# Prompt attention in five stages instead of four, with the queries normalized ahead of the logits' operations

## The chip, the core and the metric

The kernel runs on one core of a Trainium2 chip. The core has a matrix engine (TensorE, PE in the profile, with its weight loads as PEld), VectorE (DVE), ScalarE (ACT), GpSimd (POOL) and SyncE (SP), whose queue issues the DMAs. Each engine works through its own list of instructions and waits on semaphores for the others. The metric is the device time of one execution in microseconds (us), lower is better.

## The reference

One layer of a hybrid decoder, for a prompt of 2048 positions and for eight single samples. What matters here is the prompt's sliding-window attention with 16 heads of 64 in 4 groups. In short:

```python
h = rmsnorm(x, norm_g) * (1 + scale) + shift
q, k, v, ga, xr, gr, ma, mr = split(h @ w_in)           # 1024, 256, 256, 1024, 1024, 1024, 1024, 1024 columns
q = rmsnorm(q.reshape(B, T, 16, 64), q_g)                # per head
k = rmsnorm(k.reshape(B, T, 4, 64), k_g)
logits = q . k * 64**-0.5                                # keys of the own and of the previous 128-block
logits = where(0 <= dist < 128, logits + rel_bias(dist), -1e30)
p = softmax(concat(logits, sink))[..., :-1]              # one sink logit per head
o = p @ v
ya = o * silu(ga)
hs = rglru(causal_conv(xr)); yr = hs * silu(gr)
y = x + gate * ((sigmoid(ma) * (ya @ w_pa) + sigmoid(mr) * (yr @ w_pr)) @ w_out)
```

The layer also returns the last 128 keys and values, the convolution's last rows and the recurrence's last state, and the same for the samples, whose attention runs over a window of 128 cached keys.

## The kernel before

The prompt is worked through in two halves of 1024 positions, the samples along with the second. A half begins with the keys and values (`phase_kv`), goes on with the attention (`phase_attn`), and then with a long line of matmul pieces for the gates, the recurrence and the output (`stages`, `line`). Matmul operands are kept in two parts, a rounded high part and the rest, and each product is three matmuls (high by high, high by low, low by high).

The attention works on 32 tiles: 4 pairs of two heads in each of two groups (`u`) by 8 blocks of 128 positions (`tt`). Its loop is a software pipeline written out by hand: one **turn** `i` of the loop does one stage each for several tiles, and inside the attention every instruction is kept in the order in which the loop writes it, on each engine. A tile's stages are:

- `gemm_a`, `stage_a1`: 24 matmuls make the queries of tile i in a `pg` bank; ScalarE squares them, VectorE sums the squares (the **reduction**), and GpSimd makes the **factor** of the norm in two operations (`rstd_of`, the second one a power).
- `stage_a2`: VectorE's **normalization**, the queries times their factor, out of the `pg` bank into an `H` tile.
- `stage_b1`: TensorE transposes the normalized queries, ScalarE makes the high part, VectorE the low part (the **split queries**).
- `stage_b2`: 12 matmuls make the **logits** in two `pq` banks. The pool `pq` has two banks, so a tile takes both.
- `stage_b0`, `stage_b3`: GpSimd copies the sinks into a tile; then the **logits' operations** on VectorE, two masked copies and four additions of the bias with a running extreme (with an accumulator read each), and four exponentials on ScalarE.
- `stage_b4`: VectorE's **reciprocal** of the sums and GpSimd's **product** of the probabilities with it.
- `stage_c1`, `stage_c2`: transposes of the probabilities, their masked copies, and the values' matmuls.

Turn i of the loop writes, in this order: `stage_b4` of tile i - 2, splitting of weights that are due (`weights`), `stage_b0` of tile i - 1, q matmuls and `stage_a1` of tile i, `stage_b1` of tile i - 1, `stage_c1` of tile i - 3, `stage_c2` of tile i - 4, filler matmuls (`fill`), `stage_b2` and `stage_b3` of tile i - 1, `stage_a2` of tile i. The filler is the attention's gate, cut into 12 halves of 12 matmuls of 512 columns; the list `want` says how many are done by the end of each turn. The weights of the next 256 query columns are split in turns 4 to 7, 12 to 15 and 20 to 23 (one ScalarE and one VectorE operation in each), those of the last gate column group at the start of turn 31. In the last turns the loop also emits pieces of the line that follows (`line.emit`). In the second half, `stage_s` puts the samples' queries in: at the end of the turns with tt = 2, 4, 6 and 7 it issues a step of them behind the logits' operations.

Of the kernel before, what the change touches and what calls it, by code (L numbers as in the profile page):

```python
# [41 lines left out]
def tile_hybrid_step(ctx: ExitStack, tc: tile.TileContext, x_prompt, x_sample, cache_k, cache_v, state_conv,  # L42
# [27 lines left out]
    cp = ctx.enter_context(tc.tile_pool(name="cp", bufs=1))  # L70
    sp = ctx.enter_context(tc.tile_pool(name="sp", bufs=1))
    bp = ctx.enter_context(tc.tile_pool(name="bp", bufs=1))
    hp = ctx.enter_context(tc.tile_pool(name="hp", bufs=6))
    mp = ctx.enter_context(tc.tile_pool(name="mp", bufs=16))
    dp = ctx.enter_context(tc.tile_pool(name="dp", bufs=1, space=DRAM))
    pg = ctx.enter_context(tc.tile_pool(name="pg", bufs=3, space=PSUM))
# [480 lines left out]
    def phase_attn(s, hT, sa, kT, vt, chunks, line):  # L557
# [9 lines left out]
        def stage_a2(ps, ss):  # L567
            qn = H([2, 2, HD])
            V.tensor_tensor(qn, ps[:, :256].rearrange("p (gg j d) -> p j gg d", gg=2, j=2),
                            ss.rearrange("p (gg j) -> p j gg", gg=2).unsqueeze(3).broadcast_to([P, 2, 2, HD]),  # L570
                            op=ALU.mult)
            return qn

        def stage_b1(u, tt, qn):
            Gp = u // 2
            if tt == 0 and s > 0:
                kcs[u] = [H([256], F32R), H([256], F32R)]
                for kc, car, cur in zip(kcs[u], (KCh, KCl), kT[Gp]):
                    A.copy(kc[:, 0:P], car[:, Gp, :])
                    A.copy(kc[:, P:256], cur[:, 0:P])  # L580
            p2 = PT()
            for jl in range(2):
                T_.transpose(p2[:, jl * P:(jl + 1) * P], qn[:, jl].rearrange("p g d -> p (g d)"), ident)
            qh, ql = H([2, P], F32R), H([2, P], F32R)
            src = p2[:, :256].rearrange("p (j c) -> p j c", j=2)
            A.activation(qh, src, AF.Identity, scale=qg)
            V.scalar_tensor_tensor(ql, src, qg, qh.bitcast(F32), op0=ALU.mult, op1=ALU.subtract)
            return qh, ql
# [44 lines left out]
        def stage_b4(lt, sm):  # L633
            V.reciprocal(sm, sm)
            G_.tensor_tensor(lt[:, :, 0:P], lt[:, :, 0:P], sm.unsqueeze(2).broadcast_to([P, 4, P]), op=ALU.mult)
            return lt

        def stage_c1(tt, lt):
            p3 = PT().rearrange("p (h q) -> p h q", h=4)
            for i in range(4):  # L640
                T_.transpose(p3[:, i, :], lt[:, i, 0:P], ident)
            free(lt)
            pc = Tt([4, P])
            if s == 0 and tt == 0:
                V.tensor_tensor(pc, p3, mcT4, op=ALU.mult)
                return [(vt[0][0][:, 0, :], pc)]
            pa = Tt([4, P])
            A.copy(pa, p3)
            V.tensor_tensor(pc, p3, mcT4, op=ALU.mult)
            return [(v_before(vt, tt), pa), (vt[1][tt // 2][:, tt % 2, :], pc)]  # L650
# [94 lines left out]

        gps = [None]
        nh = len(GA) * nt
        want = [4, 6, 6] + [2 * nt] * (N - 4) + [nh - 2] + [nh] * 4


        order = [(next(i for i in range(N) if want[i] > n * nt) if n > 1 else max(n - 1, 0), 0, 2, "g", f, 0, h)
# [13 lines left out]
        def weights(i, end):  # L765
            while order and order[0][:2] <= (i, end):
                kind, n, _, h = order.pop(0)[3:]
                dst = (wqs if kind == "q" else wga).setdefault(n, [])
                dst.extend(split_raw(raws[0], 256 if kind == "q" else 128, halves=(h,)))
                if h == 1:  # L770
                    if s == 1 and kind == "g":
                        raw = [r_.rearrange("p (k c) -> p k c", c=128) for r_ in raws[0]]
                        gsm.append(samples_gemm([raw[k // 4][:, k % 4, :] for k in range(KT)], P, hsF,
                                                (sgaS if n < KT else maS)[:, n % KT:n % KT + 1, :], PG,
                                                PT))
                        next(gsm[-1])
                    raws.pop(0)
                    prefetch()
# [10 lines left out]
        pend = yield  # L789
        pinned[0] = True  # L790
        weights(-1, 1)
        ps_, qn_, c_, sm_, lt_ = {}, {}, {}, {}, {}
        for i in range(N + 4):
            evacs = []
            gsm_ready = len(gsm)
            if 2 <= i <= N + 1:
                lt_[i - 2] = stage_b4(*sm_.pop(i - 2))
            weights(i, 0)
            if 1 <= i <= N:
                ub, tb = seq[i - 1]  # L800
                if tb == 0 and ub % 2 == 0:
                    mbs[ub // 2] = S([8, P])
                    ld.dma_start(mbs[ub // 2], Md[:, ub // 2 * 8:ub // 2 * 8 + 8])
                lt = stage_b0(ub)

            def fill(n):
                nonlocal hdone
                while hdone < n:
                    evacs.append(ga_half(hdone))
                    hdone += 1  # L810

            if i == N:
                fill(nh - 1)
            if i > N:
                line.emit(2 * (i - N - 1))
            if i < N:
                u, tt = seq[i]
                ps_[i] = PG()
                gemm_a(ps_[i], wqs[u], hT, tt * P)
                if s == 1 and tt == 2:  # L820
                    next(smp[u])
                if tt == 7:
                    drop(wqs.pop(u))
                ss = stage_a1(ps_[i])
            if 1 <= i <= N:
                b = stage_b1(ub, tb, qn_.pop(i - 1))
            if i:
                weights(i - 1, 1)
            if 3 <= i < N + 3:
                c_[i - 3] = stage_c1(seq[i - 3][1], lt_.pop(i - 3))  # L830
            if i < N and pend:
                next(pend.pop(0))
            if i > N:
                line.emit(2 * (i - N - 1) + 1)
            if i >= 4:
                u4, t4 = seq[i - 4]
                stage_c2(u4, t4, c_.pop(i - 4))
                if u4 == 3 and t4 % 2:
                    free(vt[1][t4 // 2])
                if t4 == 7:  # L840
                    for f in (2 * u4, 2 * u4 + 1):
                        st.dma_start(yad[s, f], ya[f])
                        free(ya.pop(f))
            fill(want[i])
            if 1 <= i <= N:
                sm_[i - 1] = stage_b3(ub, tb, stage_b2(ub, tb, *b), lt)
                if ub % 2 and tb == 7:
                    free(mbs.pop(ub // 2), *kT[ub // 2])
            if i < N:
                qn_[i] = stage_a2(ps_.pop(i), ss)  # L850
            for e in evacs:
                if e:
                    e()
            if s == 1 and i < N and tt in (2, 4, 6, 7):
                next(smp[u])
            if gsm and gsm_ready:
                next(gsm.pop(0))
            if N - 7 <= i <= N:
                for t in range(2):
                    line.emit(2 * (i - N - 1) + t)  # L860
        for g in gsm:
            next(g)
        if sa is not None:
# [1233 lines left out]
```

## Time and profile before

| what | us |
|---|---|
| median of 3 runs (range) | 1991.65 (1986.59 to 1992.99) |
| the profiled execution | 1989.24 |
| its span | 1987.5 |
| TensorE busy | 1944.0 |
| VectorE busy | 1396.0 |
| ScalarE busy | 994.4 |
| GpSimd busy | 414.6 |

The profiled execution's time is 1.7 us longer than the span, which is the time from the first to the last instruction on the core. The granted clock of TensorE was 0.998 of full speed over the span. In rows of instructions in order of time, the first number is the start, the second the length, then engine, line, operation, what it writes and reads, shapes and how often; in brackets stands the idle time of the engine just before it and what ended that. All lines are 60, since one helper records every operation, so a row is told by its tiles. A row with more than one instruction runs from the first start to the last end, and TensorE's ends are modelled. In tables of stretches the numbers behind the stretch are its length, then the busy time and the instructions of TensorE, its weight loads, VectorE, ScalarE and GpSimd, the granted clock, the DMA engines' share and GB/s. The attention takes, in the first half, about 106 to 343 us of the span, and in the second about 1045 to 1295 us.

### The profile page before, as it was taken

What the parts mean: (1) busy time and instruction counts of PE and PEld (TensorE: products, weight loads), DVE (VectorE), ACT (ScalarE), POOL (GpSimd) and SP (SyncE); (2) the same over time, 40 slices, a digit from 0 to 9 for tenths busy, and PEclk for the clock granted to TensorE, in tenths of its full rate; (3) what the DMA queues carried; (4) which work ended last, traced back from release to release, by engine and by line L of the source; (5) the groups of instructions that cost most, each with busy time, mean ns of one, the idle gap of its engine ahead of it and who ended that gap; (6) DMA issues with size and microseconds to landing.
All of it is one profiled execution on the core that took longest, in us unless ns stands there. A gap on an engine that the chain in (4) does not pass through costs nothing. (4 is left out here: it accounts for less than half of the span.)

```text
span 1987.5 us, 32756 instructions
## 1 busy us (share of the span) xinstructions
PE 1944.0 (98%) x11504; PEld 1570.3 (79%) x11504; DVE 1396.0 (70%) x2942; ACT 994.4 (50%) x2279; POOL 414.6 (21%) x540
## 2 busy tenths in 40 slices
PE   6999999999999999999999999999999999999999
PEld 4788887778888878887898888777787877777777
DVE  3548877766878876588744877677677879754965
ACT  4435665345666766423423566543475767532321
POOL 4114443000201112161012444310011201111600
PEclk9999999999999999999999999999999999999999
DMA  9521114553433467986621111454233325458673
GB/s 315 173 71 41 57 54 142 164 180 102 134 102 109 146 185 239 325 278 187 227 63 46 44 54 54 123 155 144 82 114 107 128 93 169 142 167 293 220 231 110
DMA packets 307691, 286.66 MB, mean 144 GB/s; under 512 B 57073, under 2 KB 224229, under 8 KB 307486
## 3 DMA queue, kind: packets, MB, share of 16 engines
q1 hardware_dynamic: 307398, 282.41, 45.5%
q8 instruction: 91, 1.49, 0.3%
q0 software_dynamic: 128, 2.15, 0.3%
q14 instruction: 74, 0.61, 0.1%
HBM read 200.69 MB, written 85.93 MB: 144 GB/s over the span
## 5 line engine op out<-in xcount | busy, mean ns | idle before, releaser
L60 PE MATMUL pg<-S,B 128*128 128x512 f32 x4032 | 977.0, 397 | 4.8 <-DVE B L60 4.4
L60 PEld LDWEIGHTS pg<-S,B 128*128 128x128 f32 x4032 | 747.8, 188 | 190.0 <-issue 10.4
L60 DVE TENSOR_TENSOR B<-B,B 128x512 fp32r<-128x512 f32 (+1 forms) x732 | 547.9, 771 | 153.8 <-ACT B L60 143.5
L60 PE MATMUL pq<-S,B 128*128 128x512 f32 x1584 | 385.5, 397 | 7.5 <-DVE B L60 7.5
L60 POOL TENSOR_TENSOR B<-B,B 128x512 f32<-128x512 f32 x128 | 192.9, 1523 | 924.6 <-DVE B L60 504.9
L60 PEld LDWEIGHTS pq<-S,B 128*128 128x128 f32 x1584 | 295.9, 189 | 81.8 <-DVE B L60 10.9
L60 ACT CAST B<-B 128x512 fp32r<-128x512 f32 x468 | 280.3, 617 | 112.1 <-DVE B L60 71.9
L60 PE MATMUL pg<-B,S 128*128 128x256 f32 x1872 | 247.8, 288 | 2.2 <-DVE S L60 1.6
L60 PEld LDWEIGHTS pg<-B,S 128*128 128x128 f32 x1872 | 230.2, 191 | 13.6 <-ACT S L60 2.2
L60 ACT ACTIVATE B<-B,M 128x129 f32<-128x129 f32 x260 | 102.7, 396 | 151.3 <-DVE M L60 145.7
L60 ACT CAST S<-B 128x512 fp32r<-128x512 f32 x184 | 108.8, 620 | 93.0 <-DVE B L60 43.6
L60 ACT ACTIVATE B<-B 128x512 f32<-128x512 f32 (+1 forms) x150 | 93.1, 630 | 116.9 <-DVE B L60 108.9
L60 DVE TENSOR_TENSOR S<-B,S 128x512 fp32r<-128x512 f32 x184 | 141.6, 800 | 13.1 <-ACT S L60 12.7
L60 POOL TENSOR_TENSOR B<-B,M 128x512 f32<-128x512 f32 x64 | 67.1, 1049 | 221.9 <-DVE M L60 211.5
L60 DVE SCALAR_TENSOR_TENSOR B<-B,pg 128x512 f32<-128x512 f32 x78 | 53.2, 683 | 75.7 <-PE pg L60 62.3
L60 POOL TENSOR_TENSOR M<-M,mhalf 128x4 f32<-128x4 f32 (+3 forms) x102 | 96.8, 949 | 8.5
L60 DVE TENSOR_TENSOR B<-pq,B 128x512 f32<-128x512 f32 x96 | 65.9, 687 | 43.9 <-PE pq L60 37.7
L60 ACT COPY H<-pt 128x256 f32<-128x256 f32 (+1 forms) x47 | 15.6, 333 | 150.9 <-PE pt L60 150.9
L60 ACT COPY B<-pg 128x512 f32<-128x512 f32 x80 | 46.8, 585 | 88.6 <-PE pg L60 80.2
L60 DVE CUSTOM_DVE_ANT_0 B<-pq,S,skn 128x128 f32<-128x128 f32 x256 | 79.8, 350 | 4.5
L60 DVE SCALAR_TENSOR_TENSOR B<-B,VT,B 128x512 f32<-128x512 f32 x96 | 81.2, 846 | 2.3
L60 DVE COPY_PREDICATED pq<-maskf,pq 128x256 f32<-128x256 int32 x120 | 51.2, 426 | 38.6 <-PE pq L60 38.3
(198 smaller groups left out, 1794.4 us busy)
## 6 DMA issues: line engine op xcount, KB each, us to landing
B<-in_w_in_dram SPq DMA_DIRECT2D x144, 256.0 KB
B<-in_w_in_dram SPq DMA_DIRECT2D x128, 128.0 KB
B<-yad SPq DMA_DIRECT2D x56, 256.0 KB
B<-hd SPq DMA_DIRECT2D x48, 256.0 KB
B<-in_w_out_dram SPq DMA_DIRECT2D x48, 256.0 KB
S<-in_w_ada_dram SPq DMA_DIRECT2D x32, 256.0 KB
S<-in_x_prompt_dram SPq DMA_DIRECT2D x16, 512.0 KB
hd<-B SPq DMA_DIRECT2D x32, 256.0 KB
```

Of the source, the lines that this page charges most:

```text
L60: ins = fn(*args, **kw)
```

## The change

The loop gets one more stage: the split queries of `stage_b1` are kept in `qk_` and used by `stage_b2` one turn later, so logits, their operations, the product, the probabilities' transposes and the values' matmuls all move one tile back. There are N + 5 turns instead of N + 4, and the filler and the pieces of the next line are shifted to fit. Inside a turn, `stage_a2` of tile i now stands between `stage_b2` and `stage_b3`. The pool of `H` tiles has eight buffers instead of six.

```diff
-    hp = ctx.enter_context(tc.tile_pool(name="hp", bufs=6))
+    hp = ctx.enter_context(tc.tile_pool(name="hp", bufs=8))
...
-        want = [4, 6, 6] + [2 * nt] * (N - 4) + [nh - 2] + [nh] * 4
+        want = [4, 6, 6] + [2 * nt] * (N - 4) + [nh - 3, nh - 1] + [nh] * 4
...
-        ps_, qn_, c_, sm_, lt_ = {}, {}, {}, {}, {}
-        for i in range(N + 4):
+        ps_, qn_, qk_, c_, sm_, lt_ = {}, {}, {}, {}, {}, {}
+        for i in range(N + 5):
             evacs = []
             gsm_ready = len(gsm)
+            if 3 <= i <= N + 2:
+                lt_[i - 3] = stage_b4(*sm_.pop(i - 3))
+            weights(i, 0)
             if 2 <= i <= N + 1:
-                lt_[i - 2] = stage_b4(*sm_.pop(i - 2))
-            weights(i, 0)
-            if 1 <= i <= N:
-                ub, tb = seq[i - 1]
+                ub, tb = seq[i - 2]
...
-            if i == N:
-                fill(nh - 1)
-            if i > N:
-                line.emit(2 * (i - N - 1))
+            if N <= i <= N + 1:
+                fill(nh - 2 + 2 * (i - N))
+            if i > N + 1:
+                line.emit(2 * (i - N - 2))
...
             if 1 <= i <= N:
-                b = stage_b1(ub, tb, qn_.pop(i - 1))
+                qk_[i - 1] = stage_b1(*seq[i - 1], qn_.pop(i - 1))
             if i:
                 weights(i - 1, 1)
-            if 3 <= i < N + 3:
-                c_[i - 3] = stage_c1(seq[i - 3][1], lt_.pop(i - 3))
+            if 4 <= i < N + 4:
+                c_[i - 4] = stage_c1(seq[i - 4][1], lt_.pop(i - 4))
...
-            if i >= 4:
-                u4, t4 = seq[i - 4]
-                stage_c2(u4, t4, c_.pop(i - 4))
+            if i >= 5:
+                u4, t4 = seq[i - 5]
+                stage_c2(u4, t4, c_.pop(i - 5))
...
             fill(want[i])
-            if 1 <= i <= N:
-                sm_[i - 1] = stage_b3(ub, tb, stage_b2(ub, tb, *b), lt)
+            if 2 <= i <= N + 1:
+                lps = stage_b2(ub, tb, *qk_.pop(i - 2))
+            if i < N:
+                qn_[i] = stage_a2(ps_.pop(i), ss)
+            if 2 <= i <= N + 1:
+                sm_[i - 2] = stage_b3(ub, tb, lps, lt)
                 if ub % 2 and tb == 7:
                     free(mbs.pop(ub // 2), *kT[ub // 2])
-            if i < N:
-                qn_[i] = stage_a2(ps_.pop(i), ss)
...
-            if N - 7 <= i <= N:
+            if N - 6 <= i <= N + 1:
                 for t in range(2):
-                    line.emit(2 * (i - N - 1) + t)
+                    line.emit(2 * (i - N - 2) + t)
```

On VectorE, one turn of the first half before, from the last bias addition of the logits' operations (ISA, with its accumulator read) to the next turn's first masked copy (COPY_PREDICATED):

```order
L60 ISA B_2798,M_2868<-pq_2855,S_1511,skn_950 128x128
L60 ISA M_2868 128x1
L60 TENSOR_TENSOR H_2880<-pg_2800,M_2827 128x256
L60 RECIPROCAL M_2875<-M_2875 128x4
L60 TENSOR_REDUCE M_2913<-H_2911 128x4
L60 SCALAR_TENSOR_TENSOR H_2921<-pt_2917,qg_944,H_2920 128x256
L60 TENSOR_TENSOR B_2929<-pt_2924,mcT_90 128x512
L60 COPY_PREDICATED pq_2940<-maskf_88,pq_2940 128x2x128
```

The normalization (H_2880, from a pg bank) stands behind the logits' operations and ahead of the reciprocal; the reduction (M_2913), the queries' low part (H_2921) and the masked copy of the probabilities (B_2929) follow.

On VectorE, the same place in the changed kernel:

```order
L60 ISA B_2838,M_2910<-pq_2895,S_1591,skn_950 128x128
L60 ISA M_2910 128x1
L60 RECIPROCAL M_2917<-M_2917 128x4
L60 TENSOR_REDUCE M_2953<-H_2951 128x4
L60 SCALAR_TENSOR_TENSOR H_2961<-pt_2957,qg_944,H_2960 128x256
L60 TENSOR_TENSOR B_2969<-pt_2964,mcT_90 128x512
L60 TENSOR_TENSOR H_2994<-pg_2926,M_2953 128x256
L60 COPY_PREDICATED pq_2980<-maskf_88,pq_2980 128x2x128
```

The normalization (H_2994) now stands ahead of the first masked copy, in the turn whose reduction (M_2953) it depends on.

On GpSimd, the rows of the changed kernel between that reciprocal and that normalization:

```order
L60 TENSOR_TENSOR B_2838<-B_2838,M_2917 128x4x128
L60 COPY B_2924<-skn_950 128x4
L60 TENSOR_SCALAR M_2953<-M_2953 128x4
L60 TENSOR_TENSOR M_2953<-M_2953,mhalf_94 128x4
L60 TENSOR_TENSOR B_2924<-B_2924,M_3003 128x4x128
```

The product with the reciprocal (M_2917), the copy of the sinks, and the two operations of the factor (M_2953), then the next turn's product: the same sequence as before, in which nothing moved.

More of the change, by code (lines that the diff above doesn't have):

```diff
@@ L825, in phase_attn @@
             if 1 <= i <= N:
-                b = stage_b1(ub, tb, qn_.pop(i - 1))
+                qk_[i - 1] = stage_b1(*seq[i - 1], qn_.pop(i - 1))
             if i:
                 weights(i - 1, 1)
-            if 3 <= i < N + 3:
-                c_[i - 3] = stage_c1(seq[i - 3][1], lt_.pop(i - 3))
+            if 4 <= i < N + 4:
+                c_[i - 4] = stage_c1(seq[i - 4][1], lt_.pop(i - 4))
             if i < N and pend:
                 next(pend.pop(0))
-            if i > N:
-                line.emit(2 * (i - N - 1) + 1)
-            if i >= 4:
-                u4, t4 = seq[i - 4]
-                stage_c2(u4, t4, c_.pop(i - 4))
+            if i > N + 1:
+                line.emit(2 * (i - N - 2) + 1)
+            if i >= 5:
+                u4, t4 = seq[i - 5]
+                stage_c2(u4, t4, c_.pop(i - 5))
                 if u4 == 3 and t4 % 2:
```

## The prediction

> **What bounds it now.** I read the page first, then a table of two stretches of the attention, then TensorE's instructions in order of time there, and last VectorE's and GpSimd's in the same stretches.
>
> ```profile
> span 1987.5 us, 32756 instructions
> ...
> PE 1944.0 (98%) x11504; PEld 1570.3 (79%) x11504; DVE 1396.0 (70%) x2942; ACT 994.4 (50%) x2279; POOL 414.6 (21%) x540
> ```
>
> TensorE is busy for 1944.0 of 1987.5 us. The change adds no work and takes none away, so it can only move TensorE's waits: at most 43.5 us can be won, and only a wait that is made can be lost. The two stretches below run from the start of turn 4's q matmuls to the start of turn 30's logits, one for each half.
>
> ```profile
> 146.45:301.36 154.91, 152.38 (x1324) 128.29 (x1322) 125.94 (x434) 92.33 (x343) 68.46 (x108) 1.00 0.16 49
> 1088.05:1249.22 161.17, 160.26 (x1394) 135.81 (x1392) 127.44 (x447) 98.47 (x365) 72.68 (x116) 1.00 0.15 47
> ```
>
> TensorE seems to idle there for only 2.5 and 0.9 us. More is hidden in the modelled ends of its rows: the starts tell it. Between 217.41 and 223.04 lies a turn without a wait, 5.63 us from one group of 24 q matmuls to the next; 211.47 to 217.41 takes 5.94, because the 12 logits matmuls take until 1.24 after their start instead of 0.90.
>
> ```profile
> 211.47 3.09 PE L60 MATMUL pg<-B,S 128*128 128x256 f32 x24
> ...
> 216.17 1.31 PE L60 MATMUL pq<-S,H 64*128 64x256 f32 x12
> 217.41 3.12 PE L60 MATMUL pg<-B,S 128*128 128x256 f32 x24
> ...
> 221.12 0.66 PE L60 MATMUL pt<-B,S 128*64 128x256 f32 x4
> ...
> 222.14 0.97 PE L60 MATMUL pq<-S,H 64*128 64x256 f32 x12
> 223.04 3.12 PE L60 MATMUL pg<-B,S 128*128 128x256 f32 x24
> ```
>
> What they wait for is the low part of the split queries, made by VectorE in the same turn:
>
> ```profile
> 134.97 1.38 PE L60 MATMUL pq<-S,H 64*128 64x256 f32 x12 [0.78 <-ACT H L60]
> ...
> 245.36 0.51 PE L60 MATMUL pq<-S,H 64*128 64x256 f32 x4 [0.48 <-DVE H L60]
> ...
> 1076.93 1.02 PE L60 MATMUL pq<-S,H 64*128 64x256 f32 x12 [0.62 <-ACT H L60]
> ```
>
> The first stretch is 26 turns and 4.73 us of a 27th (217.41 to 222.14). Without waits that is 26 x 5.63 + 4.73 = 151.1 us, against 154.9: about 3.8 us of waits; I take as much for the second, which has the samples' matmuls in it. That, and the waits at 134.97 and 1076.93 ahead of the stretches, 0.78 + 0.62 = 1.4 us, is all that the change can take away in the attention: 2 x 3.8 + 1.4 = 9.0 us.
>
> **What the change removes.** The logits of tile i - 2 now use queries split one turn earlier, so these waits go. The extra turn costs no TensorE work: the gate's halves and the next stage's pieces move along with it. Eight H buffers instead of six cover the split tiles that live one turn longer (four H tiles a turn, two turns), so I price the buffers at nothing; were one short, ScalarE's square would wait for the turn's logits, 0.9 us at most, under 3 us of q matmuls.
>
> **What it moves, and the cost.** The normalization of tile i now stands ahead of the logits' operations in VectorE's order. GpSimd's order has not changed: the probabilities' product, a small copy, then the two operations that make the normalization's factor. These are the rows of one plain turn.
>
> ```profile
> 223.14 0.43 DVE L60 COPY_PREDICATED pq<-maskf,pq 128x256 f32<-128x256 int32 x1 [0.61 <-PE pq L60]
> ...
> 225.16 0.42 DVE L60 TENSOR_TENSOR H<-pg,M 128x256 f32<-128x256 f32 x1
> 225.93 0.18 DVE L60 RECIPROCAL M<-M 128x4 f32<-128x4 f32 x1 [0.34 <-ACT B L60]
> ...
> 226.18 1.04 POOL L60 TENSOR_TENSOR B<-B,M 128x512 f32<-128x512 f32 x1 [3.08 <-DVE M L60]
> 227.17 0.19 POOL L60 COPY B<-skn 128x4 f32<-128x4 f32 x1
> 227.44 0.19 POOL L60 TENSOR_SCALAR M<-M 128x4 f32<-128x4 f32 x1
> 227.72 1.01 POOL L60 TENSOR_TENSOR M<-M,mhalf 128x4 f32<-128x4 f32 x1
> ...
> 228.69 0.49 DVE L60 COPY_PREDICATED_SCALAR pq<-maskf,bigc 128x256 f32 x1 [0.48 <-PE pq L60]
> ```
>
> Before, the normalization (225.16) comes after the logits' operations (223.14 to 225.16) and its factor has long been there. Now it is the other way round, and a ring closes in which TensorE has no part: normalization, logits' operations, exponentials on ScalarE, reciprocal, product on GpSimd, copy, factor, next normalization. VectorE's and GpSimd's orders let none of them pass another. Behind a waiting normalization stand all of the tile's logits' operations, and for those wait ScalarE's exponentials, GpSimd's product and TensorE, which needs the logits' buffers back. One lap:
>
> - reciprocal to product: 225.93 to 226.18, 0.25
> - product, copy, first factor operation: 226.18 to 227.72, 1.54
> - start of the second factor operation to the normalization: 1.04, from the rows below
> - normalization: 0.42 (225.16), after which the logits' operations start
> - first logits' operation to the reciprocal: 223.14 to 225.93, 2.79; the reciprocal waits for ScalarE's exponentials, not for the normalization that stood between
>
> Sum 6.04 us, against TensorE's 5.63. The slack now is nil already: the factor is ready at 227.72 + 1.04 = 228.76, and the logits' operations begin at 228.69.
>
> ```profile
> 88.41 0.42 DVE L60 TENSOR_TENSOR H<-pg,M 128x256 f32<-128x256 f32 x1
> 88.75 0.34 DVE L60 SCALAR_TENSOR_TENSOR S<-pt,VT,S 128x128 fp32r<-128x128 f32 x1
> ...
> 105.38 1.01 POOL L60 TENSOR_TENSOR M<-M,mhalf 128x4 f32<-128x4 f32 x1
> ...
> 106.42 0.42 DVE L60 TENSOR_TENSOR H<-pg,M 128x256 f32<-128x256 f32 x1 [1.41 <-POOL M L60]
> ```
>
> The pair at 105.38 and 106.42 gives the 1.04, and shows the same normalization holding VectorE for 1.41 us with nothing passing it. The pair at 88.41 gives the other bound of the normalization: the next instruction started 0.34 after it. I take the row's own 0.42, since the operation behind it reads PSUM as the normalization does; 0.34 would make a lap 5.96.
>
> The Trainium skill, "TensorE: Matmul & The Clock Gate", in the section on the array's architectural detail, says that VectorE's queue is strictly first in, first out. By that rule the 1.41 us wait is what a late factor must cost, and the change pays in every turn; if the logits' operations could pass the normalization, the change would win its 9 us. The row agrees with the rule.
>
> In 12 turns of each half a half of the next q weights is split (turns 4 to 7, 12 to 15, 20 to 23), between reciprocal and reduction:
>
> ```profile
> 202.48 0.18 DVE L60 RECIPROCAL M<-M 128x4 f32<-128x4 f32 x1 [0.34 <-ACT B L60]
> 202.99 1.33 DVE L60 TENSOR_TENSOR B<-B,B 128x512 fp32r<-128x512 f32 x1 [0.33 <-ACT B L60]
> 204.25 0.41 DVE L60 TENSOR_REDUCE M<-H 128x4 f32<-128x256 f32 x1
> ...
> 203.72 0.65 POOL L60 COPY B<-skn 128x4 f32<-128x4 f32 x1
> 204.74 0.19 POOL L60 TENSOR_SCALAR M<-M 128x4 f32<-128x4 f32 x1 [0.37 <-DVE M L60]
> 205.02 1.01 POOL L60 TENSOR_TENSOR M<-M,mhalf 128x4 f32<-128x4 f32 x1
> ```
>
> There the factor waits for the reduction: 202.48 to 205.02 is 2.54, then 1.04 + 0.42 + 2.79: a lap of 6.79.
>
> From the first logits' operation of turn 3 to that of turn 29 are 26 laps, 12 with a split: 12 x 6.79 + 14 x 6.04 = 166.0 us. TensorE writes the logits into the two buffers of one pool, so turn 30's logits start when turn 29's logits' operations end, 2.0 us later (223.14 to 225.16): 168.0 us for the stretch that takes 154.9 now, +13.1. The values' matmuls of one tile (221.12 to 222.14, 1.0; half of it for the first tile of all) leave turn 4 and are done behind the stretch: +0.5 in the first half, +1.0 in the second.
>
> The second half has the eight samples' queries too, whose operations stand on VectorE ahead of the reciprocal:
>
> ```profile
> 1134.70 0.41 DVE L60 TENSOR_TENSOR H<-pg,H 8x256 f32<-8x256 f32 x1 [0.73 <-ACT H L60]
> 1135.05 0.15 DVE L60 RECIPROCAL M<-M 128x4 f32<-128x4 f32 x1
> ...
> 1143.10 0.43 DVE L60 COPY_PREDICATED pq<-maskf,pq 128x256 f32<-128x256 int32 x1
> ...
> 1146.52 0.15 DVE L60 RECIPROCAL M<-M 128x4 f32<-128x4 f32 x1
> ...
> 1149.77 1.01 POOL L60 TENSOR_TENSOR M<-M,mhalf 128x4 f32<-128x4 f32 x1
> ...
> 1150.82 0.42 DVE L60 TENSOR_TENSOR H<-pg,M 128x256 f32<-128x256 f32 x1
> ```
>
> The addition at 1134.70 makes the reciprocal start 0.7 late (0.73 of idle and 0.35 in place of 0.34): three laps, 2.2 us. The samples' normalization makes it 1143.10 to 1146.52 = 3.42 instead of 2.79, and their factor ahead of the product makes it 4.30 from reciprocal to normalization (1146.52 to 1150.82) instead of 2.54 + 1.04 = 3.58 in a split lap or 2.83 in a plain one. Three split laps at 1.35 and one plain at 2.1: 6.15. So 168.0 + 8.35 = 176.4 against 161.2: +15.2.
>
> Turn 31 then starts the merge gate's weights. They are split behind the reciprocal:
>
> ```profile
> 305.17 0.18 DVE L60 RECIPROCAL M<-M 128x4 f32<-128x4 f32 x1 [0.34 <-ACT B L60]
> 305.67 1.94 DVE L60 TENSOR_TENSOR B<-B,B 128x512 fp32r<-128x512 f32 x2 [0.33 <-ACT B L60]
> ...
> 306.96 5.84 PE L60 MATMUL pg<-S,B 128*128 128x512 f32 x24
> ```
>
> Counted from the start of turn 30's logits (the end of turn 29's logits' operations), turn 30's logits' operations begin at 6.04 - 2.0 = 4.04, turn 31's reciprocal comes at 4.04 + 2.79 = 6.83 and the first low half 0.50 + 1.33 later, at 8.66. TensorE is there at 0.90 + 4.73 = 5.63 and can do two of the twelve matmuls without the low half (2 x 5.84/24 = 0.49): it waits 2.5 us, in each half. If ScalarE's part alone held it, nothing would be waited for; that is the lower bound, 0. From there on the gate's matmuls make TensorE's turns longer than 8 us and it sets the pace again.
>
> Sum: 13.1 + 0.5 + 15.2 + 1.0 + 2 x 2.5 - 1.4 = **+33.4 us**, on the profiled execution's 1989.24 us: 2022.6. That execution lies 2.4 us under the median of the runs, 1991.65, and inside their range, 1986.59 to 1992.99. I forecast **2023 us**.
>
> **Bounds.** Low: laps of 0.08 less (52 x 0.08 = 4.2), the gate's wait 0 (-5.0), the samples' operations hidden (-8.35): +16, 2005 us. High: the copy on GpSimd takes 0.65 in each plain lap, as it does at 203.72, instead of 0.19: 28 x 0.46 = 12.9, so 2036. The likeliest case's own range is 2005 to 2036.
>
> The Trainium skill, "SBUF — State Buffer", in the section "Who interferes with whom", says that a VectorE instruction with two SBUF inputs contends with a GpSimd one that reads SBUF, and one with a single SBUF input does not. Only the weights' split is of that kind in a turn, and 0.65 beside it against 0.19 at 227.17 agrees. By this rule the high bound is not reached.
>
> **Rivals.**
> 1. *The ring is not closed*: GpSimd's last operation ends earlier than its row says (the page calls spans on GpSimd rough), so a lap stays under 5.63. Then all 9.0 us are won: 1980 us. It takes 0.41 off a lap. For it: the logits' waits that go are real. Against: at 106.42 the consumer itself started 1.04 after, and 1150.82 follows 1149.77 by 1.05. 7%.
> 2. *It cancels*: laps of 5.75 on average instead of 6.39 (33.4 / 52 = 0.64 less), for instance because the exponentials start earlier when VectorE has just idled. 1989 us. Against: the 2.79 is VectorE's own work and two exponentials behind it, with 0.34 idle. 5%.
> 3. *Slower still*: every lap costs as one with a split, because the wait shifts GpSimd's product onto two-input operations: 28 x 0.75 = 21 us more, 2044 us. The change's place would be the same, the price double. For it: 1.33 for one split at 202.99. Against: the orders of the two engines around the product have not changed. 8%.
> 4. *The two logits buffers bind instead*: logits' operations, then TensorE's 0.90, then the next: 2.0 + 0.9 = 2.9 us, under any lap; the logits' wait then changes its releaser, and no number.
>
> **Numbers.** 80% for the forecast. A measurement of this kernel tells 0.3%, 6 us, from no change. Faster has rival 1 and a little of 2: 0.08; same 0.05; slower 0.87. The range 2005 to 2036 holds nearly all of the forecast's cases and a little of rival 3.
>
> **What would show it.** In the changed kernel the logits should no longer wait for the split queries but for VectorE's reads of the pool's buffers. VectorE's normalization should be released by GpSimd, and the idle time before it be 0.9 us or more in each plain turn. The starts of turns should lie 6.0 apart, 6.8 with a split. Turn 31's gate matmuls should wait once for VectorE. The stretches outside the attention should keep their times within 2 us. I am wrong if the turns lie 5.6 apart: then the ring is open somewhere, and rival 1 holds; if normalizations wait but turns are longer than 6.3 without a split, a price on GpSimd is wrong.

## The result, and the profile after

The changed kernel takes 2022.07 us (median of four runs, 2019.49 to 2025.52) against 1991.81 for the kernel before: a ratio of 1.0158, 95% interval 1.0134 to 1.0182. It is 30 us slower, and the forecast was 2023 us. The page of the changed kernel has nearly the same busy times as the page before (15.6 us more on TensorE, whose ends are modelled, and 5.3 us less on ScalarE), and a longer span:

```profile
span 2023.8 us, 32812 instructions
...
PE 1959.6 (97%) x11504; PEld 1582.4 (78%) x11504; DVE 1397.5 (69%) x2942; ACT 989.1 (49%) x2279; POOL 415.4 (21%) x540
```

Tables of stretches, for the kernel before and then for the changed one. The stretches are: 20 us ahead of the attention, and for each half the attention from the 48 gate matmuls that open it to the short gate piece of 0.63 us behind its last turns.

```profile
60.00:80.00 20.00, 18.66 (x158) 16.71 (x158) 10.25 (x43) 9.43 (x20) 1.24 (x2) 1.00 0.88 269
109.84:352.56 242.72, 237.62 (x1805) 195.94 (x1804) 177.67 (x554) 128.89 (x452) 93.13 (x135) 0.99 0.22 68
1049.90:1301.84 251.94, 250.11 (x1998) 207.59 (x1997) 178.69 (x575) 137.45 (x481) 96.44 (x143) 1.00 0.22 68
```

```profile
60.00:80.00 20.00, 16.50 (x119) 14.69 (x118) 6.92 (x24) 8.62 (x18) 0.00 (x0) 0.83 0.76 251
113.73:370.79 257.06, 244.20 (x1805) 199.95 (x1804) 178.55 (x554) 125.50 (x452) 93.08 (x135) 0.99 0.21 64
1067.82:1338.03 270.21, 254.66 (x1997) 211.63 (x1996) 179.09 (x575) 135.69 (x481) 96.49 (x143) 0.98 0.21 63
```

The first half's attention went from 242.72 to 257.06 us (+14.3), the second's from 251.94 to 270.21 (+18.3): together +32.6. Between the halves (697.34 before, 697.03 after) and behind the second (685.66 and 685.77) nothing changed. The profiled execution of the changed kernel is 36.3 us longer than that of before, not 32.6, because its attention starts 3.9 us later: between 60 and 80 us TensorE did less, at a granted clock of 0.83 instead of 1.00. The only thing that the change alters there is the size of the pool of `H` tiles, and the starts do not go by it: the kernels below start the attention at 109.8 to 114.8 with six buffers and at 108.2 to 114.0 with eight (what sets it off was not tried). So I compare the attention's stretches, each from one execution, beside the medians of the runs; by the medians the change costs 30.3 us, by the two profiled attentions 32.6.

Inside the attention the ring is there. VectorE's and GpSimd's rows of a split turn's end and a plain turn (in brackets the idle time ahead and what ended it):

```profile
221.82 0.18 DVE L60 RECIPROCAL M<-M 128x4 f32<-128x4 f32 x1 [0.68 <-ACT B L60]
...
225.40 0.42 DVE L60 TENSOR_TENSOR H<-pg,M 128x256 f32<-128x256 f32 x1 [0.42 <-POOL M L60]
...
228.51 0.18 DVE L60 RECIPROCAL M<-M 128x4 f32<-128x4 f32 x1 [0.68 <-ACT B L60]
228.76 1.04 POOL L60 TENSOR_TENSOR B<-B,M 128x512 f32<-128x512 f32 x1 [3.40 <-DVE M L60]
...
230.30 1.01 POOL L60 TENSOR_TENSOR M<-M,mhalf 128x4 f32<-128x4 f32 x1
231.34 0.42 DVE L60 TENSOR_TENSOR H<-pg,M 128x256 f32<-128x256 f32 x1 [1.04 <-POOL M L60]
231.68 0.42 DVE L60 COPY_PREDICATED pq<-maskf,pq 128x256 f32<-128x256 int32 x1
...
234.45 0.18 DVE L60 RECIPROCAL M<-M 128x4 f32<-128x4 f32 x1 [0.68 <-ACT B L60]
```

From the reciprocal at 228.51 to the next at 234.45 are 5.94 us, from 221.82 to 228.51, with a split, 6.69. These two lengths come back all through the first half's 26 laps: 6.69 to 6.70 in eleven of the twelve with a split, 5.94 to 5.96 in eleven of the fourteen without. The normalization (231.34) starts 1.04 after the factor's second operation (230.30), and VectorE had been idle for 1.04 until then. Groups of waits in the first half's stretch (turn 4's q matmuls to turn 30's logits), VectorE's and TensorE's: us in total, how often, the longest.

```profile
DVE H L60 <- POOL M L60: 17.1, 22, 1.1
...
PE pt L60 <- DVE H L60: 7.8, 11, 0.7
PE pq L60 <- DVE M L60: 1.1, 4, 0.3
```

VectorE waits 22 times in 26 turns for GpSimd's factor, 17.1 us in all. TensorE's wait now comes from the transposes (pt), for the normalized queries, and hardly from the logits' buffers (pq). Turn 31's gate, with the operands that hold it in brackets:

```profile
321.46 0.73 PE L60 MATMUL pg<-S,B 128*128 128x512 f32 x2 [1.20 <-ACT B L60]
322.83 2.58 PE L60 MATMUL pg<-S,B 128*128 128x512 f32 x10 [0.64 <-DVE B L60]
```

### The profile page after: what moved, and what is told of

Same layout as the page of the kernel before. It is cut to its first block, busy times and chain, and to the rows that moved or that the text cites. A ratio compares the mean times of both kernels' runs of the same rounds, so it can differ in the third digit from the quotient of the medians.

```text
span 2023.8 us, 32812 instructions
## 1 busy us (share of the span) xinstructions
PE 1959.6 (97%) x11504; PEld 1582.4 (78%) x11504; DVE 1397.5 (69%) x2942; ACT 989.1 (49%) x2279; POOL 415.4 (21%) x540
## 5 line engine op out<-in xcount | busy, mean ns | idle before, releaser
L60 PEld LDWEIGHTS pq<-S,B 128*128 128x128 f32 x1584 | 297.3, 189 | 82.1 <-DVE B L60 10.7
L60 ACT COPY H<-pt 128x256 f32<-128x256 f32 (+1 forms) x47 | 15.6, 332 | 150.2 <-PE pt L60 150.2
L60 PE MATMUL pt<-ident,H 128*128 128x128 f32 (+2 forms) x258 | 52.6, 280 | 22.6 <-DVE H L60 18.4
```

Source lines behind the costliest of these rows:

```text
L60: ins = fn(*args, **kw)
```

## The experiments

The table gives each one's attention in the two halves, taken from its profile between the same two places as above, the sum against before, and the runs. A ratio is that of a kernel's runs to runs of the kernel before made along with them, whose median was between 1988.93 and 1991.81 us.

| kernel | 1st half, us | 2nd half, us | sum against before | median, us | ratio, 95% interval |
|---|---|---|---|---|---|
| before | 242.72 | 251.94 | | 1991.81 | |
| changed | 257.06 | 270.21 | +32.6 | 2022.07 | 1.0158 (1.0134 to 1.0182) |
| order alone | 257.02 | 270.10 | +32.5 | 2022.05 | 1.0163 (1.0147 to 1.0179) |
| stage alone | 240.84 | 250.71 | -3.1 | 1988.55 | 0.9984 (0.9975 to 0.9994) |
| changed, two more copies | 267.82 | 280.83 | +54.0 | 2043.43 | 1.0273 (1.0254 to 1.0291) |
| before, two more copies | 242.61 | 252.24 | +0.2 | 1990.54 | 1.0002 (0.9992 to 1.0012) |
| changed, product behind | 237.53 | 256.44 | -0.7 | 1986.89 | 0.9985 (0.9975 to 0.9994) |
| changed, splits behind | 255.11 | 266.39 | +26.8 | 2017.77 | 1.0150 (1.0136 to 1.0165) |
| changed, both behind | 235.09 | 248.86 | -10.7 | 1980.93 | 0.9953 (0.9939 to 0.9966) |
| before, splits behind | 237.54 | 250.06 | -7.1 | 1984.01 | 0.9968 (0.9956 to 0.9981) |
| stage alone, splits behind | 237.32 | 251.29 | -6.1 | 1982.95 | 0.9964 (0.9949 to 0.9978) |
| before, both behind | 236.69 | 248.15 | -9.8 | 1982.18 | 0.9966 (0.9954 to 0.9977) |
| stage alone, both behind | 236.44 | 248.12 | -10.1 | 1981.91 | 0.9965 (0.9951 to 0.9979) |

### The order alone

The kernel before, with only the normalization put ahead of the logits' operations:

```diff
             if 1 <= i <= N:
-                sm_[i - 1] = stage_b3(ub, tb, stage_b2(ub, tb, *b), lt)
...
+                lps = stage_b2(ub, tb, *b)
             if i < N:
                 qn_[i] = stage_a2(ps_.pop(i), ss)
+            if 1 <= i <= N:
+                sm_[i - 1] = stage_b3(ub, tb, lps, lt)
...
```

> The kernel before, with only the normalization of tile i put between the logits' matmuls and the logits' operations of tile i - 1: four stages as before, six buffers. Theory (order alone closes the ring): laps of 5.95 in plain turns and 6.7 in split turns, as in the changed kernel; the first half's stretch takes 165 to 169 us against 154.9, the time is 2022 us (2014 to 2030). Rival A (the additional stage is what costs): 1992 us, no change. Rival C (the normalization ahead costs only together with the additional stage, since then the logits lie ready early): between them, 1992 to 2010 us.

Measured: 2022.05 us, 1.0163, and both halves within about 0.1 us of the changed kernel's. VectorE's rows of a plain lap, and the groups of TensorE's waits in the first half:

```profile
231.57 0.18 DVE L60 RECIPROCAL M<-M 128x4 f32<-128x4 f32 x1 [0.68 <-ACT B L60]
...
234.40 0.42 DVE L60 TENSOR_TENSOR H<-pg,M 128x256 f32<-128x256 f32 x1 [1.04 <-POOL M L60]
...
237.51 0.18 DVE L60 RECIPROCAL M<-M 128x4 f32<-128x4 f32 x1 [0.68 <-ACT B L60]
...
PE pq L60 <- DVE H L60: 6.3, 11, 0.7
PE pq L60 <- ACT H L60: 5.9, 13, 1.1
```

The lap is the same 5.94 (231.57 to 237.51), with the same 1.04 us of idle ahead of the normalization, but here TensorE waits at the logits, for the split queries. So the order alone makes the whole loss, in any number of stages; at which of its operations TensorE is then held is only where the loss shows. Rival A and rival C fall.

### The additional stage alone

The changed kernel with the normalization put back:

```diff
-            if i < N:
-                qn_[i] = stage_a2(ps_.pop(i), ss)
             if 2 <= i <= N + 1:
                 sm_[i - 2] = stage_b3(ub, tb, lps, lt)
...
+            if i < N:
+                qn_[i] = stage_a2(ps_.pop(i), ss)
```

> The changed kernel with the normalization of tile i put back behind the logits' operations of tile i - 2: the additional stage, the eight buffers and the shifted filler stay. Theory (the ring through VectorE, ScalarE and GpSimd is closed by the order inside the turn alone): the ring is open, the logits' waits for the split queries stay away, turns start 5.6 apart in both halves, the stretch from turn 4's q matmuls to turn 30's logits takes 151 to 152 us in the first half, turn 31's gate does not wait, and the time is 1983 us (1979 to 1988), 9 us under the kernel before. Rival A (the additional stage itself costs, by its longer-lived buffers and its last turn): about 2022 us, as the changed kernel. Rival B (the waits that the stage takes away were hidden by others): 1990 to 1993 us, no change.

Measured: 1988.55 us, 0.9984. The ring is open and the loss is gone, which refutes rival A; but the gain is 3.1 us in the attention, not 9. The expectation of 1983 was a miss: the time lies between it and rival B's 1990 to 1993, and of the 9 us forecast two thirds did not come, as rival B had it. TensorE still waits in the split turns. The group of its waits in the first half's stretch, then one transposition on TensorE and VectorE's rows around it:

```profile
PE pt L60 <- DVE H L60: 3.8, 7, 1.0
...
162.62 0.41 PE L60 MATMUL pt<-ident,H 128*128 128x128 f32 x2 [0.96 <-DVE H L60]
...
162.81 0.18 DVE L60 RECIPROCAL M<-M 128x4 f32<-128x4 f32 x1 [0.34 <-ACT B L60]
163.32 1.33 DVE L60 TENSOR_TENSOR B<-B,B 128x512 fp32r<-128x512 f32 x1 [0.33 <-ACT B L60]
...
169.05 0.18 DVE L60 RECIPROCAL M<-M 128x4 f32<-128x4 f32 x1 [0.34 <-ACT B L60]
```

From reciprocal to reciprocal are 6.24 us (162.81 to 169.05), of which VectorE idles 0.34 and 0.33, both for ScalarE. So a split turn of VectorE, with a split of 1.33 and these two waits, is longer than TensorE's turn of 5.63; in the later split turns, where VectorE no longer multiplies the outputs by the gate, it is 5.85 (reciprocals at 209.56 and 215.41). Those waits belonged to VectorE's turn, and one more stage between split queries and logits did not take them away.

### Two more copies on GpSimd, in either kernel

```diff
-            G_.tensor_copy(lt[:, :, 128:129], skn[:, u * 4:u * 4 + 4].unsqueeze(2))
+            for _ in range(3):
+                G_.tensor_copy(lt[:, :, 128:129], skn[:, u * 4:u * 4 + 4].unsqueeze(2))
```

> The changed kernel with GpSimd's small copy of the sinks done three times instead of once, ahead of the factor: two more operations of 0.27 to 0.28 us each in every turn, on an engine that is busy for a fifth of the span. Theory (the ring of VectorE, ScalarE and GpSimd sets the pace, and this copy is a piece of it): a plain lap goes from 5.95 to 6.5 us, a split lap, in which the factor waits for the reduction besides, by 0.2 to 0.5; first half +10 to +13, second half +6 to +12, 2038 to 2046 us. Rival (VectorE's wait comes from something else, and GpSimd's small operations are hidden): no change, 2020 to 2025 us.

> The same two additional copies per turn in the kernel before, as the control. Theory: there the factor has about 2 us until the normalization behind the logits' operations needs it, so nothing is waited for: 1988 to 1994 us, no change. Rival (any work on GpSimd costs, through the memory it shares with VectorE or through its own length): 2005 us or more.

Measured: 2043.43 us in the changed order, 21.4 us more than the changed kernel; 1990.54 in the old order, a ratio of 1.0002. VectorE's and GpSimd's rows of a plain turn, changed order:

```profile
228.35 0.18 DVE L60 RECIPROCAL M<-M 128x4 f32<-128x4 f32 x1 [0.68 <-ACT B L60]
229.59 0.69 POOL L60 COPY B<-skn 128x4 f32<-128x4 f32 x3
...
231.69 0.42 DVE L60 TENSOR_TENSOR H<-pg,M 128x256 f32<-128x256 f32 x1 [1.54 <-POOL M L60]
...
234.80 0.18 DVE L60 RECIPROCAL M<-M 128x4 f32<-128x4 f32 x1 [0.68 <-ACT B L60]
```

The idle time ahead of the normalization went from 1.04 to 1.54, the lap from 5.94 to 6.45 (228.35 to 234.80), and the two halves by 10.8 and 10.6 us. GpSimd is busy for 22% of the span there. The same work costs nothing measurable where its result is not waited for, and its full length of 0.50 in each plain lap where it stands in the ring.

### The product behind the factor

```diff
         def stage_b4(lt, sm):
             V.reciprocal(sm, sm)
+            return lt, sm
+
+        def stage_b5(lt, sm):
             G_.tensor_tensor(...)
...
                 ss = stage_a1(ps_[i])
+            if 3 <= i <= N + 2:
+                lt_[i - 3] = stage_b5(*lt_[i - 3])
```

The product is now `stage_b5` (its operands are left out here), written behind the factor of `stage_a1`.

> The changed kernel with GpSimd's product of the probabilities issued behind the two operations of the factor instead of ahead of them; nothing else moves. Theory (the lap is made of the pieces in a row: product 1.04 and its handoff leave it): a plain lap would be 0.34 + 2.79 + some 0.7 for reciprocal and reduction + 0.28 + 1.04 = 5.1 us, under TensorE's 5.63, so plain turns start 5.63 apart; a split lap becomes about 6.1 instead of 6.69 (reciprocal, split, reduction on VectorE, then the factor), part of it covered by the plain turns' slack; 24 split laps at up to 0.45: 1983 to 1994 us. Rival D (a normalization in front of the logits' operations costs by itself, whatever stands on GpSimd): about 2022 us. Rival E (the product's place does not matter because the reduction, not the product, holds the factor): 2015 us or more.

Measured: 1986.89 us. With the normalization still ahead, the product's 1.04 out of the ring is enough to win the 33 us back, so rivals D and E fall. A split lap is 6.04 (expected 6.1), and a plain one 5.22:

```profile
164.18 0.18 DVE L60 RECIPROCAL M<-M 128x4 f32<-128x4 f32 x1 [0.68 <-ACT B L60]
164.69 0.69 DVE L60 TENSOR_TENSOR B<-B,B 128x512 fp32r<-128x512 f32 x1 [0.33 <-ACT B L60]
...
168.04 0.19 POOL L60 COPY B<-skn 128x4 f32<-128x4 f32 x1
...
170.22 0.18 DVE L60 RECIPROCAL M<-M 128x4 f32<-128x4 f32 x1 [0.68 <-ACT B L60]
175.44 0.18 DVE L60 RECIPROCAL M<-M 128x4 f32<-128x4 f32 x1 [0.68 <-ACT B L60]
```

The split now takes 0.69 and the copy 0.19 in the same turn; beside the product they took 1.33 and 0.65. Four split laps of 6.04 to 6.06 are longer than TensorE's 5.63, but the four plain laps behind them (5.20 to 5.33) make up for it, and TensorE has no wait left in the first half's stretch. Against the kernel before, the first half is 5.2 us shorter and the second still 4.5 us longer (256.44 against 251.94); there TensorE waits three times for 1.5 us at the samples' transposes. What makes up the 4.5 us was not worked out.

### The splits behind the split queries too

```diff
-            weights(i, 0)
+            if not (i % 8 >= 4 and i < 24):
+                weights(i, 0)
```

In these turns the call of `weights` behind `stage_b1`, which is there already, now does the splitting.

> As the kernel with the product behind the factor, and in turns 4 to 7, 12 to 15 and 20 to 23 the splitting of the next q weights (one operation on ScalarE and one on VectorE) is written behind the split queries instead of at the start of the turn, so that it stands no longer between reciprocal and reduction. Theory: a split lap loses the split's 0.5 to 1.3 us and falls to 5.1 to 5.6, so no turn of the first half is set by the ring: 1980 to 1986 us, the first half's stretch 151 to 152 us. Rival (split laps are long because the split holds VectorE, wherever it stands): no gain against the kernel with the product behind alone. Rival D: about 2022 us.

Measured: 1980.93 us, 0.9953: the fastest here, 9 us under the 1989.98 of before in the same comparison. VectorE's rows of a split turn:

```profile
202.07 0.18 DVE L60 RECIPROCAL M<-M 128x4 f32<-128x4 f32 x1 [0.68 <-ACT B L60]
...
203.21 0.69 DVE L60 TENSOR_TENSOR B<-B,B 128x512 fp32r<-128x512 f32 x1
...
207.53 0.18 DVE L60 RECIPROCAL M<-M 128x4 f32<-128x4 f32 x1 [0.68 <-ACT B L60]
```

The lap is 5.46 (202.07 to 207.53), shorter than TensorE's turn, with the split at 0.69 and no wait for the factor; TensorE has no wait left in the first half's stretch. In turns 4 to 7, where VectorE also multiplies the outputs by the gate, it is 5.84. The first half's stretch took 148.2 us, under the expected 151 to 152, in part because these still counted the values' matmuls that the stage moves out of turn 4.

### The splits behind, the product ahead

The edit of the splits on the changed kernel, with the product left ahead of the factor.

> The changed kernel with only the q weights' splitting moved behind the split queries; GpSimd's product stays ahead of the factor. Theory (a split lap was 6.69 because the split stood between reciprocal and reduction): the reduction no longer holds the factor, so split laps fall to the plain 5.95, or to 6.4 if the split now runs beside the sinks' copy and stretches it from 0.19 to 0.65; the ring stays closed in every turn. 24 laps at 0.3 to 0.74 less: 2004 to 2015 us, still slower than before. Rival (the split's place was the whole loss): 1990 us or less. Rival (the split's place has no part in it): 2020 to 2025 us.

Measured: 2017.77 us, just outside the expected 2004 to 2015. VectorE's rows of a split turn, and GpSimd's copy:

```profile
207.27 0.18 DVE L60 RECIPROCAL M<-M 128x4 f32<-128x4 f32 x1 [0.68 <-ACT B L60]
208.41 0.71 DVE L60 TENSOR_TENSOR B<-B,B 128x512 fp32r<-128x512 f32 x1
208.51 0.66 POOL L60 COPY B<-skn 128x4 f32<-128x4 f32 x1
...
210.57 0.42 DVE L60 TENSOR_TENSOR H<-pg,M 128x256 f32<-128x256 f32 x1 [0.85 <-POOL M L60]
...
213.68 0.18 DVE L60 RECIPROCAL M<-M 128x4 f32<-128x4 f32 x1 [0.68 <-ACT B L60]
```

The lap is 6.41 (207.27 to 213.68): the upper of the two values that I had named, with the copy at 0.66 beside the split. 24 laps at 0.28 less are 6.7, and the attention gained 5.8. The runs' ratio, 1.0150, does not tell this from the changed kernel's 1.0158; the laps do. The ring stays closed with the split out of it; the split's place is a small part.

### Without the change: what the moves are worth by themselves

The splits' edit on the kernel before and on the stage alone, and both edits on each.

> The kernel before, four stages and the old order of the normalization, with only the splitting of the next q weights in turns 4 to 7, 12 to 15 and 20 to 23 written behind the split queries instead of at the start of the turn. Theory (the logits' waits in those turns are VectorE's whole turn, 5.94 us from reciprocal to reciprocal with 0.67 of waits for ScalarE and a split of 1.33 beside GpSimd's product, and not the handing over of the split queries): the reduction and the queries' low part come earlier, the split runs partly after the product and is shorter, turns fall to 5.65, and 24 turns at up to 0.3 are won: 1982 to 1986 us. Rival (the waits come from splitting queries and using them in one turn, which only one more stage removes): 1989 to 1992 us, no change.

> The additional stage with the normalization behind the logits' operations (no ring), and the q weights' splitting behind the split queries; GpSimd's product stays ahead of the factor. Theory: what held the kernel with the additional stage alone at 5.85 to 6.24 us in split turns was VectorE's queue, so these fall to 5.6 to 5.8: 1979 to 1984 us, like the kernel with product and splits both behind (1980.9). Rival (the gain of that kernel came from the product's new place, with the normalization ahead): 1986 to 1990 us, like the additional stage alone.

> Four stages and the old order of the normalization, with the q weights' splitting behind the split queries and GpSimd's product behind the factor: the best changed kernel's two moves without the change. Theory (the moves help by shortening VectorE's turn, and the factor was never late in this order, so the product's place adds little): 1981 to 1985 us. Rival (the product's place is worth 3 us or more in any order): 1980 us or less. Rival (the additional stage and the early normalization are needed for it): 1985 us or more.

> The additional stage, the normalization behind the logits' operations, and both moves (splits and product behind). Theory: the ring is open in either order of the normalization once the product is behind, so this differs from the kernel with the early normalization (1980.9) by less than 3 us: 1979 to 1984 us. Rival (the early normalization is worth something by itself, because TensorE's transposes get the normalized queries 2 us earlier): 1984 us or more.

Measured: 1984.01, 1982.95, 1982.18 and 1981.91 us. In the kernel before, with four stages, the splits' place alone takes 7.1 us out of the attention; in the first half's split turns TensorE's logits no longer wait. VectorE's rows of one of them:

```profile
205.30 0.18 DVE L60 RECIPROCAL M<-M 128x4 f32<-128x4 f32 x1 [0.34 <-ACT B L60]
...
206.63 0.69 DVE L60 TENSOR_TENSOR B<-B,B 128x512 fp32r<-128x512 f32 x1
...
210.69 0.18 DVE L60 RECIPROCAL M<-M 128x4 f32<-128x4 f32 x1 [0.34 <-ACT B L60]
```

This lap is 5.39 (205.30 to 210.69), the shortest of the four from turn 12 on; the other three are 5.58 to 5.61, TensorE's pace, where the kernel before had 5.94 to 5.96. So most of the waits for the split queries in the kernel before came from VectorE's split at the wrong place. With both moves made, four stages (-9.8), five stages with the old order (-10.1) and with the new one (-10.7) lie within 1 us in the attention, and their ratios' intervals overlap: once both moves are made, neither the additional stage nor the early normalization adds anything that these runs can tell. All four lie inside what the theory had expected. In the kernel before, the product's place takes another 2.8 us out of the attention of one execution (7.06 to 9.82); the ratios, 0.9968 and 0.9966, do not tell the two apart.

## Why the prediction was right, point by point

- **The ring** was right in its place and its pieces. The order alone gives the loss, opening the ring at another place undoes it, and lengthening one piece lengthens the lap by that. Reciprocal to product 0.25, product to the factor's second operation 1.54 and from there to the normalization 1.04 are the values predicted. In each of the 22 turns of the first stretch in which the normalization waited, VectorE's next instruction was the masked copy behind it, 0.34 to 0.35 after the normalization's start: nothing passed.
- **The plain lap** was 5.94 to 5.96 in eleven of fourteen, predicted 6.04: the term *normalization: 0.42* was mis-sized. The logits' operations started 0.34 after it (231.34 to 231.68), which was the low bound. A split lap was 6.69 instead of 6.79, mostly for the same reason. Against that, the other three plain laps took 6.06 to 6.07, and the first of the 26 laps took 1.1 more, since the gate's operation on VectorE (150.84, behind a wait of 1.16 for ScalarE) stood ahead of the reciprocal; the sum had neither.
- **The sum.** The first stretch took 166.77 us, predicted 168.0. With the stretch behind it, the half's attention is +14.3; the prediction's terms for it (13.1 + 0.5 + 2.5 - 0.78) make 15.3. The second half is +18.3 against 15.2 + 1.0 + 2.5 - 0.62 = 18.1.
- **Turn 31's gate** waited 1.20 + 0.64 in the first half (the rows at 321.46 and 322.83), and 0.81 + 0.64 in the second; the term *it waits 2.5 us* was too large, 3.3 in all instead of 5.0, and the larger part of it is a wait for ScalarE's part, which the prediction's lower bound had taken to hold nothing.
- **What the change removes** was wrong. I put 9.0 us of TensorE's waits down to the split queries and called that all that could be won. The stage alone won 3.1; the rest were split turns in which VectorE's turn is longer than TensorE's. The 3.8 us taken over for the second half was not read from it either: TensorE's waits for the split queries in its stretch before were two, 0.6 us together. It did not enter the sum but for 1.4 us, since the ring set those turns anyway. But rival 1's 1980 us did not come out with the ring open by the order: 1988.55.
- **The sign *the logits wait for VectorE's reads of the pool's buffers*** was wrong: 1.1 us of such waits, against 7.8 for transposes that wait for the normalized queries. I had followed the logits' buffers and not the other thing that TensorE needs from VectorE in each turn. So the 2.0 us added for turn 30's logits had the wrong reason.
- **The second half's number was right by cancelling.** I added the samples' extra operations to 26 full laps. In fact TensorE's own samples' matmuls made some turns long enough for VectorE to catch up, and after them three turns in a row went at 5.6 us (q matmuls at 1151.99, 1157.58, 1163.19 and 1168.79). The loss came instead in turns like the one at 1168.79, 9.3 us long: the samples' factor stood on GpSimd ahead of the product, VectorE waited 2.09 for the factor behind it, and TensorE ran slowly after its own wait. VectorE's, GpSimd's and TensorE's rows:

```profile
1169.38 1.32 POOL L60 TENSOR_TENSOR M<-M,mhalf 8x4 f32<-8x4 f32 x1
1170.68 1.03 POOL L60 TENSOR_TENSOR B<-B,M 128x512 f32<-128x512 f32 x1
...
1173.25 0.42 DVE L60 TENSOR_TENSOR H<-pg,M 128x256 f32<-128x256 f32 x1 [2.09 <-POOL M L60]
...
1173.83 0.51 PE L60 MATMUL pt<-ident,H 128*128 128x128 f32 x2 [1.93 <-DVE H L60]
```

- **Outside the attention** the times stayed within 0.3 us, but for the start, where the clock differed.
- **The total** came out nearer than its parts: 2023 against 2022.07. The sum of +33.4 was put on an execution of 1989.24 us, which lies 2.6 us below the median that the change is measured against; between the medians it is +30.3. That these two errors nearly cancel is luck, and so is the second half's sum; the ring and its lap are not.

## What to carry to other kernels

Before an instruction is moved forward on an engine that works in order, follow what it waits for back through the other engines' lists until the chain comes round: if it meets its own engine, the lap time of that ring is a lower bound on the mean turn, however little each engine is busy. Such a ring can be opened at the engine with room, by putting its urgent operation ahead of a long one that nobody waits for (here GpSimd's product behind the factor: 35 us between the medians from one exchange). And a wait of the busiest engine for a small operation should be checked against the whole turn of the engine that makes it, before a buffer or a stage is added: here moving the split behind two small operations of VectorE did what a further stage could not.

## What the runs showed of the hardware

**TensorE's clock fell behind some waits of 1.56 to 2.22 us.** A stretch of transposes to the next turn's q matmuls took 2.66 us at a granted clock of 1.00, and 4.26 us at 0.60 behind the wait of 1.93:

```profile
1166.13:1168.79 2.66, 2.66 (x28) 1.85 (x26) 1.64 (x10) 2.27 (x10) 0.00 (x0) 1.00 0.98 350
1173.83:1178.09 4.26, 4.26 (x26) 2.68 (x27) 3.18 (x12) 3.52 (x14) 1.47 (x2) 0.60 0.24 85
...
1131.58 0.28 PE L60 MATMUL pt<-ident,H 8*128 8x8 f32 x2 [2.22 <-DVE H L60]
1131.79 4.51 PE L60 MATMUL pg<-B,S 128*128 128x256 f32 x24
```

The same happened at 1131.79, where 24 q matmuls took 4.51 us instead of 3.10 behind a wait of 2.22, and at 1237.94 (4.62, behind a wait of 1.56); the granted clock over these two groups was 0.64 and 0.63. Behind waits of 2.09 (at 1119.62) and 2.06 (at 1226.51) it stayed at 1.00. The three cost about 1.4 + 1.6 + 1.5 = 4.5 us, which the prediction did not have. The Trainium skill, "TensorE: Matmul & The Clock Gate", in the section "Why this matters for your kernels", gives idle gaps of more than about 3 us between bursts as what drops the clock. These rows show a drop after 1.56 to 2.22 us of idle, in some cases and not in others; here the measurement decides, and what sets the difference between the cases was not tried.

**VectorE and GpSimd in turn.** A split (VectorE, two inputs from SBUF) took 1.33 us when it started beside the product and 0.69 to 0.71 where it did not, in the rows above. GpSimd's 0.19 us copy took 0.65 to 0.66 when it started beside a split, in the kernel before, in the changed one and with the splits behind (208.51), where the split, first this time, kept 0.71. The one that starts second ends only after the other: in the changed kernel the split that started at 158.26 ended 0.55 after the product's end at 159.04, and the copy at 208.51 ended 0.05 after the split. The Trainium skill, "SBUF — State Buffer", in the section "Who interferes with whom", describes this as an exclusive lock on a shared pair of ports, which a VectorE instruction with two SBUF inputs contends for with a GpSimd instruction that reads SBUF; the trace agrees. The prediction used this rule, without the exception that the page makes for VectorE's 2-port modes, to say that a copy of 0.65 would not be met in plain turns, and it wasn't (0.19 in the turns without a split).
